# Moving a kernel's stores to ScalarE's DMA queue and its first small load to SP's queue

## The chip, the cores and the metric

The kernel runs on one core of one Trainium2 chip. A core has engines with an instruction stream each: TensorE (PE, not used here), VectorE (DVE in the profile), ScalarE (ACT), GpSimd (POOL) and SyncE (SP). Transfers between the chip's main memory (HBM) and the on-chip memory of 128 partitions are carried out by 16 DMA engines. An instruction stream issues a transfer and goes on; two of the streams issue transfers here, SP and ScalarE, and each has a DMA queue of its own. The metric is the time of one execution in microseconds (us) on the device.

## The reference

```python
def setup_inputs():
    batch, dim = 1024, 4096
    return {"x": np.random.randn(batch, dim).astype(np.float32), "axis": -1}

def reference(x, axis):
    mean = np.mean(x, axis=axis, keepdims=True)
    return ((x - mean) ** 2).astype(np.float32)
```

For each of 1024 rows of 4096 numbers the mean is taken, and each number becomes its squared distance from that mean. The input is 16.78 MB and so is the output.

## The kernel before, in words

The 1024 rows are cut into two tiles of 512 rows. In a tile each of the 128 partitions holds four whole rows (`Q = 4`), 16384 numbers or 64 KiB, which lie in one run in HBM as well. Both tiles have a buffer of their own, so no load waits for a store.

All loads are issued at the start (L46 to L53). Tile 0 comes in two transfers: the first 512 numbers of each partition (`HEAD`, 2 KiB) from ScalarE's queue on L51, the other 15872 from SP's queue on L52. Tile 1 comes in one transfer from SP's queue, right behind (L52 again).

Then a loop goes over the tiles. ScalarE takes the mean of row 3 (`mean_on_act`, L60: a scaled copy whose sum is accumulated). VectorE takes the means of rows 0, 1 and 2 (`mean_on_dve`: a reduction on L68 and a scaling of its 128 results on L71). ScalarE squares the rows in place, with the negated mean as a bias (`square_on_act`, L75), in the order 3, 0, 1 and then the first 9/16 of row 2; VectorE does the other 7/16 of row 2 in two instructions (L90 adds the negated mean, L91 squares). Last, one transfer stores the whole tile from SP's queue (L92).

The program's order is kept on each engine (`keep_in_program_order` for the instructions marked with it). SP's stream therefore is: rest of tile 0 in, tile 1 in, tile 0 out, tile 1 out. SP waits before each store until both compute engines are done with that tile. VectorE's first reduction of tile 0 waits for both transfers of that tile, since row 0 begins in the one and ends in the other; ScalarE's first mean needs only the larger. On tile 1 both wait for its one transfer.

## Time and profile before

| | |
|---|---|
| median of 3 runs (lowest, highest) | 83.39 us (83.36, 83.63) |
| profiled execution, its own time | 83.39 us |
| its span | 81.6 us |
| VectorE busy | 33.4 us (41%) |
| ScalarE busy | 34.7 us (43%) |
| bytes moved, mean rate over the span | 33.55 MB, 411 GB/s |
| tile 0: first VectorE instruction, store issued | 22.90 us, 39.85 us |
| tile 1: first VectorE instruction, store issued | 42.03 us, 59.0 us |

Times in the trace are counted from the start of the span. L12 stands for line 12 of the kernel. A name such as `x_tile<-in_x_dram` says what is written and what is read. An engine's name with a q (SPq, ACTq) is its instruction stream, where transfers are issued. In the list of DMA issues the last number is the median time from issue to landing, and landing is when all 16 DMA engines' completion writes for that transfer have arrived. In the table by stretches the columns after the length are the busy time of VectorE, ScalarE and GpSimd with the number of instructions, the granted TensorE clock, the mean busy share of the 16 DMA engines, and GB/s.

### The profile page before, as it was taken

To read this page: it belongs to the slowest core of one execution; us is meant where nothing else is said; L and a number is where in the kernel's file an instruction comes from. 1 tells how busy PE (TensorE), PEld (TensorE's weight loads), DVE (VectorE), ACT (ScalarE), POOL (GpSimd) and SP (SyncE) were. 2 spreads that over 40 slices of the span, in tenths; PEclk is the share of its full clock that TensorE was granted. 3 is DMA by queue.
4 is the path that set the end of the run, shared out by engine and by line. 5 is a ranking of instruction groups with operands and counts; after the bars stand their busy time and mean duration, and the time that the engine had idled before them with its cause. 6 is when DMAs were issued, how large, how long until landed. Compare 5 with 4: busy or idle time off the path is not lost.

```text
span 81.6 us, 83 instructions
## 1 busy us (share of the span) xinstructions
DVE 33.4 (41%) x16; ACT 34.7 (43%) x13; POOL 0.2 (0%) x4
## 2 busy tenths in 40 slices
DVE  0000000000079999999439999999800000000000
ACT  4100000000089999999339999999800000000000
POOL 0000000000000000000000000000000000000000
DMA  9099947999992999994899992999994799998590
GB/s 467 31 514 514 514 195 319 514 514 514 530 418 128 482 514 514 514 482 193 353 514 514 514 482 128 418 514 514 514 514 193 321 514 514 514 514 353 225 450 0
DMA packets 720, 33.55 MB, mean 411 GB/s; under 512 B 80, under 2 KB 80, under 8 KB 208
## 3 DMA queue, kind: packets, MB, share of 16 engines
q1 hardware_dynamic: 576, 33.29, 95.2%
q10 hardware_dynamic: 144, 0.26, 0.8%
HBM read 16.78 MB, written 16.78 MB: 411 GB/s over the span
## 4 chain that ended last, share of the span: by engine, by line
DMA 50%; DVE 21%; SPq 0%; issue 0%
DMA x_tile<-in_x_dram 50%; DVE neg_sum L68 16%; DVE x_tile L91 2%; DVE x_tile L90 1%; DVE neg_mean L71 1%; SPq L52 0%
## 5 line engine op out<-in xcount | busy, mean ns | idle before, releaser
L68 DVE TENSOR_REDUCE neg_sum<-x_tile 128x1 f32<-128x4096 f32 x6 | 26.5, 4412 | 25.1 <-DMA x_tile<-in_x_dram 25.1
L75 ACT ACTIVATE x_tile<-x_tile,neg_mean 128x4096 f32<-128x4096 f32 (+1 forms) x8 | 26.0, 3323 | 0.1
L60 ACT ACTIVATE copy<-x_tile 128x4096 f32<-128x4096 f32 x2 | 7.2, 3617 | 22.8 <-DMA x_tile<-in_x_dram 22.8
L91 DVE TENSOR_TENSOR x_tile<-x_tile 128x1792 f32<-128x1792 f32 x2 | 4.0, 2025 | 0.1
L90 DVE TENSOR_SCALAR x_tile<-x_tile,neg_mean 128x1792 f32<-128x1792 f32 x2 | 2.3, 1153 | 0.1
L60 ACT ACT_TABLE_LOAD x1 | 1.3, 1283 | 1.1 <-PEq L109 1.1
L71 DVE TENSOR_SCALAR neg_mean<-neg_sum 128x1 f32<-128x1 f32 x6 | 0.9, 154 | 0.2
L60 ACT ACTIVATION_READ_ACCUMULATOR copy<-x_tile 128x1 f32 x2 | 0.4, 186 | 0.0
L109 POOL MEMSET const-bfloat16-1.0<- 128x1 bf16 x1 | 0.1, 101 | 0.0
L109 POOL MEMSET const-uint8-127<- 128x1 uint8 x1 | 0.1, 101 | 0.0
L109 POOL MEMSET const-float32-0.0<- 128x1 f32 x1 | 0.1, 98 | 0.2 <-issue 0.2
L109 POOL MEMSET const-float32-1.0<- 128x1 f32 x1 | 0.1, 98 | 0.0
## 6 DMA issues: line engine op xcount, KB each, us to landing
x_tile<-in_x_dram SPq DMA_DIRECT2D x1, 7936.0 KB, 21.9
x_tile<-in_x_dram ACTq DMA_DIRECT2D x1, 256.0 KB, 22.1
out_dram<-x_tile SPq DMA_DIRECT2D x2, 21.7
x_tile<-in_x_dram SPq DMA_DIRECT2D x1, 40.8
```

Source lines behind the costliest of these rows:

```text
L60: nc.scalar.activation(out=copy, in_=row, func=ACT.Identity, scale=-inv_d, accum_out=neg_mean)
L68: inorder(nc.vector.reduce_sum(out=neg_sum, in_=row, axis=mybir.AxisListType.X, negate=True))
L71: inorder(nc.vector.tensor_scalar_mul(out=neg_mean, in0=neg_sum, scalar1=inv_d))
L75: inorder(nc.scalar.activation(out=part, in_=part, func=ACT.Square, bias=neg_mean, scale=1.0))
L90: nc.vector.tensor_scalar_add(out=back, in0=back, scalar1=m2)
L91: nc.vector.tensor_mul(out=back, in0=back, in1=back)
L109: nc = _bacc.Bacc("TRN2", target_bir_lowering=False, num_devices=1)
```

## The change

The 2 KiB head of tile 0 is no longer issued by ScalarE; SP issues it ahead of the rest of tile 0, so that SP's stream holds all three loads and nothing else. Both stores are issued by ScalarE in place of SP. In ScalarE's stream the store of tile 0 stands between its last activation of tile 0 and its first of tile 1; the store of tile 1 is its last instruction. As SP did, ScalarE waits before each store until VectorE's part of the tile is done.

```diff
     for i in range(ntiles):
         x_tile = io.tile([P, Q * D], F32)
-        lo = 0
-        if i == 0:
-            lo = HEAD
-            nc.scalar.dma_start(out=x_tile[:, :lo], in_=x_t[i][:, :lo])
-        nc.sync.dma_start(out=x_tile[:, lo:], in_=x_t[i][:, lo:])
+        cuts = [0, HEAD, Q * D] if i == 0 else [0, Q * D]
+        for lo, hi in zip(cuts, cuts[1:]):
+            nc.sync.dma_start(out=x_tile[:, lo:hi], in_=x_t[i][:, lo:hi])
         tiles.append(x_tile)
...
         nc.vector.tensor_mul(out=back, in0=back, in1=back)
-        nc.sync.dma_start(out=out_t[i], in_=tiles[i])
+        nc.scalar.dma_start(out=out_t[i], in_=tiles[i])
```

## The prediction

> **What bounds the kernel now.** I read the page's DMA parts first, since both compute engines are busy for only two fifths of the span (41% and 43%), then the DMA share by stretches, then the instructions in order of time, and last the packet records behind the DMA view (each DMA engine's packets with start, length, queue and size), which I tell in words. From the page, the packets, the queues and the issues:

> ```profile
> DMA packets 720, 33.55 MB, mean 411 GB/s; under 512 B 80, under 2 KB 80, under 8 KB 208
> q1 hardware_dynamic: 576, 33.29, 95.2%
> q10 hardware_dynamic: 144, 0.26, 0.8%
> x_tile<-in_x_dram SPq DMA_DIRECT2D x1, 7936.0 KB, 21.9
> x_tile<-in_x_dram ACTq DMA_DIRECT2D x1, 256.0 KB, 22.1
> out_dram<-x_tile SPq DMA_DIRECT2D x2, 21.7
> ```

> The DMA share (next to last column) in four stretches: load of tile 0, load of tile 1, store of tile 0, store of tile 1.

> ```profile
> 1.75:21.60 19.85, 0.00 (x0) 0.68 (x1) 0.00 (x0) 1.00 1.00 418
> 21.70:41.00 19.30, 16.71 (x8) 16.72 (x6) 0.00 (x0) 1.00 1.00 433
> 41.10:60.50 19.40, 16.71 (x8) 16.72 (x6) 0.00 (x0) 1.00 1.00 432
> 60.50:79.90 19.40, 0.00 (x0) 0.00 (x0) 0.00 (x0) 1.00 1.00 432
> ```

> The share is 1.00 in each: the DMA engines run from 1.75 us to the end without a gap, so the kernel is a DMA stream of 33.55 MB. It stays gapless for one reason, seen in the instructions in order of time (start, length):

> ```profile
> 39.85 0.35 SPq L92 DMA_DIRECT2D out_dram<-x_tile  x1
> 42.03 4.42 DVE L68 TENSOR_REDUCE neg_sum<-x_tile 128x1 f32<-128x4096 f32 x1 [2.25 <-DMA x_tile<-in_x_dram]
> ...
> 56.89 2.03 DVE L91 TENSOR_TENSOR x_tile<-x_tile 128x1792 f32<-128x1792 f32 x1
> 58.99 0.34 SPq L92 DMA_DIRECT2D out_dram<-x_tile  x1
> ```

> Store 0 is issued at 39.85, while load 1 still runs (its completion writes are at 41.00 to 41.56 on the sixteen engines, the last landing at 42.01). Tile 1's compute runs from 42.03 to 58.92, store 1 is issued at 59.0, and store 0's data end at 60.53 to 61.11. Store 1's descriptors thus wait about half a microsecond for the engines: that is all the slack there is. Whatever delays tile 1's landing by more than that opens a gap in the stream.

> **The change part by part.** *Head on SP's queue.* ScalarE loses a 0.39 us issue at 0.73; it then waits for data until 22.70, so this is worth nothing. SP issues the head at 0.73, the big part at about 1.11, tile 1 at about 1.5 (issues take 0.38 to 0.43). An SP issue at 0.73 had its first packet at 1.75, a lag of 1.02, so the big part could start at 2.13; the head's eight packets per engine (8 x 0.084 = 0.67) fill that time, and on one queue load 1 followed load 0 without a gap. The head's 0.67 us is paid as before, only first instead of in between. I take 0. Bounds: -0.29, if the head is wholly inside the wait (0.38 - 0.67); +0.74, if the big part pays the queue's cold start again (first 62 KB packet 3.08 against 2.34). VectorE, which waited for the head's own completion (landing 22.87, q1's 22.67), starts tile 0 0.20 earlier, at 22.70 as ScalarE does; its last instruction then ends at 39.58 instead of 39.78.

> *Store 0 on ScalarE's queue.* ScalarE's last activation of tile 0 ends at 39.45 (37.25 + 2.20). It now waits 0.13 for VectorE's 39.58, and issues the store at 39.65 (0.07 after VectorE, as SP did). Queued behind it on ScalarE is only tile 1's mean, which cannot start before 42.0; the 0.39 us issue is hidden there with 2 us to spare. SP's queue is moved past nothing: it has only loads left. What does move is the store's packets, from behind load 1 in q1 to q10, beside it. They reach the engines at 39.65 + 1.02 = 40.67 (lag of the load) or 39.65 + 1.27 = 40.92 (upper bound from the store: issued at 39.85, first packet 41.12). Load 1's last data packets end at 41.00 to 41.56, after both. So when such a packet ends it is q10's turn: a 64 KB store packet (2.46 us, first of its kind) goes ahead of load 1's 4-byte completion write, as the head's 2 KB packet did at tile 0. The first store packets ended at up to 44.16 in this trace; completion then, plus 0.45 to landing (41.56 to 42.01), is 44.61; without the 0.12 switch gap seen there it is 44.47. Tile 1 lands at about 44.54, 2.53 late. The data are there in time; only the message is late.

> *Store 1.* Tile 1's work keeps its 16.97 us from landing to issue, so the store is issued at 59.0 + 2.53 = 61.53. First packets at +1.02 on the first engine, +1.21 on fifteen and +1.44 on the last (first packets of load 0: 1.75 to 1.94, and 2.17): 62.55 to 62.97. But the engines have been empty since 60.5 to 61.1, a new gap of almost 2 us. Eight packets, 2.46 + 7 x 2.42 = 19.40, end at 82.37 on the last engine, against 80.46 now: +1.91. An idle queue's first store packet is not in the trace. Bounds: nothing more, or the load's largest cold start (3.44 - 2.34 = 1.10). I take the 0.12 of the store's own first packet, nearest in kind. The stagger's low end (no late sixteenth engine) makes the sum 1.7, the upper lag and cold start 1.91 + 0.25 + 1.06 = 3.2. The tail after the last landing (80.81 to 81.6) stays.

> *Sum*: 0 + 1.91 + 0.12 = +2.0. Span 81.6 + 2.0 = 83.6; the profiled execution is 83.39 with 1.79 around its span, equal to the median of the three runs (83.39), so 85.4 us.

> [...]

> **The rivals.** *The completion is not overtaken* (83.4, no change). For it: at tile 0 both queues had been filled long before, while here the store arrives only 0.1 to 0.9 us before load 1's data end, and an engine may have picked its next item by then. Against it: one overtaken engine of sixteen is enough, since the waiter needs all, and the latest ends (41.56) leave 0.6 us and more. Then nothing else in the stream changes.

> *The head on SP's queue starts the stream sooner, and nothing is overtaken* (83.39 - 0.29 = 83.1, faster). It decides only if small packets begin before the big transfer could, and the completion keeps its place. Against it: the first packet waited 1.02 us whatever came after.

> *ScalarE's queue starts a transfer more slowly than SP's.* The trace bounds its lag only by 1.02 and 3.93 (head issued at 0.73, its first packet at 4.66, held up by turns). From 1.91 on (41.56 - 39.65) the store comes too late to overtake, but starts late itself: nothing at that point, +2.5 at 3.93, say 84.6.

> *Two store packets go ahead of the completion*: another 2.42, 87.8. Against it: the turns at tile 0 were one for one throughout.

> **How the numbers follow.** Overtaken as described 0.74; not overtaken 0.14; sooner start 0.05; slow queue 0.04; two packets 0.03. A measurement of this kernel tells about 0.3% (0.25 us) from no change. Faster 0.05; same 0.14; slower 0.74 + 0.04 + 0.03 = 0.81. The likeliest case's own range is 83.39 + 1.7 - 0.3 = 84.8 to 83.39 + 3.2 = 86.6. That holds about 0.67 of the chance; to leave out no more than 0.2, the range goes down to 83.3 and takes in the unchanged case.

> **What would show it.** Right: the store's issue on ScalarE at about 39.65; tile 1's first VectorE and ScalarE instructions at about 44.5 instead of 42.03, waiting for the load; load 1's issue to landing at some 43 us instead of 40.8, with its bytes moved by 41.6; ScalarE's store issue at 61.5; a dip in the DMA strip near 61 to 62.5; q10 carrying 16.78 MB. Wrong: tile 1 starting at 42.0 with a gapless stream (not overtaken); tile 0 landing before 22.3 (a sooner start); a gap at 41 to 43 (slow queue); tile 1 starting near 47 (two packets).

## The result and the profile after

The changed kernel takes 83.88 us (median of 6 runs, 83.82 to 83.98), the kernel before 83.55 (6 runs, 83.36 to 83.66): a ratio of 1.0043, 95% interval 1.0027 to 1.0059. It is slower, as forecast, but by 0.4% and not by the 2.4% of the forecast 85.4 us. The likeliest case did not happen, so the direction came true by another cause than the forecast's. The profiled execution took 83.98 us with a span of 82.2.

From the page of the changed kernel, queues and DMA issues:

```profile
q10 hardware_dynamic: 288, 16.78, 48.1%
q1 hardware_dynamic: 432, 16.78, 48.0%
...
x_tile<-in_x_dram SPq DMA_DIRECT2D x1, 7936.0 KB, 21.4
x_tile<-in_x_dram SPq DMA_DIRECT2D x1, 256.0 KB, 2.8
out_dram<-x_tile ACTq DMA_DIRECT2D x2, 22.5
x_tile<-in_x_dram SPq DMA_DIRECT2D x1, 40.3
```

q10 carries the stores, so the change does what it says, and the head lands after 2.8 us in place of 22.1. Tile 1's load took 40.3 us to land. The forecast needed 43. The line that moved the wrong way is the third: a store takes 22.5 us from issue to landing where it took 21.7.

The instructions in order of time, around tile 1 of the changed kernel:

```profile
39.61 0.38 ACTq L90 DMA_DIRECT2D out_dram<-x_tile  x1
41.91 4.42 DVE L66 TENSOR_REDUCE neg_sum<-x_tile 128x1 f32<-128x4096 f32 x1 [2.38 <-DMA x_tile<-in_x_dram]
...
56.77 2.03 DVE L89 TENSOR_TENSOR x_tile<-x_tile 128x1792 f32<-128x1792 f32 x1
58.88 0.34 ACTq L90 DMA_DIRECT2D out_dram<-x_tile  x1
```

Store 0 is issued at 39.61 (forecast 39.65), tile 1 starts at 41.91 (forecast 44.5; before 42.03), store 1 is issued at 58.88. Nothing is late, and yet the span of the profiled execution is 0.6 us longer (82.2 against 81.6; the medians of the runs are 0.33 us apart). The packet records show where:

```
first store packet, 16 engines     starts          length, lowest/median/highest   ends
before                             41.12..41.69    2.451/2.459/2.466               43.58..44.16
changed kernel                     41.05..41.54    3.088/3.237/3.466               44.32..44.77
```

Load 1's data end at 41.54 in place of 41.56 on the last engine. The store's first packet then takes 3.24 us instead of 2.46, and all fifteen after it 2.418 (2.42 before). The last store data end at 80.99 against 80.46. The 0.5 us more is what is left of this longer packet after a vanished gap of 0.12 us ahead of it and some thousandths in each later packet.

So there are two questions: why was the completion write not overtaken, and what is the long first packet?

### The profile page after: what moved, and what is told of

It reads as the page before. It is cut to its first block, busy times and chain, and to the rows that moved or that the text cites. A ratio compares the mean times of both kernels' runs of the same rounds, so it can differ in the third digit from the quotient of the medians.

```text
span 82.2 us, 82 instructions
## 1 busy us (share of the span) xinstructions
DVE 33.4 (41%) x16; ACT 34.7 (42%) x13; POOL 0.2 (0%) x4
## 2 busy tenths in 40 slices
DMA packets 720, 33.55 MB, mean 408 GB/s; under 512 B 80, under 2 KB 80, under 8 KB 208
## 3 DMA queue, kind: packets, MB, share of 16 engines
q10 hardware_dynamic: 288, 16.78, 48.1%
q1 hardware_dynamic: 432, 16.78, 48.0%
HBM read 16.78 MB, written 16.78 MB: 408 GB/s over the span
## 4 chain that ended last, share of the span: by engine, by line
DMA 49%; DVE 20%; SPq 1%; issue 0%
DMA x_tile<-in_x_dram 49%; DVE neg_sum L66 16%; DVE x_tile L89 2%; DVE x_tile L88 1%; SPq L50 1%; DVE neg_mean L69 1%
## 6 DMA issues: line engine op xcount, KB each, us to landing
x_tile<-in_x_dram SPq DMA_DIRECT2D x1, 7936.0 KB, 21.4
x_tile<-in_x_dram SPq DMA_DIRECT2D x1, 256.0 KB, 2.8
out_dram<-x_tile ACTq DMA_DIRECT2D x2, 22.5
x_tile<-in_x_dram SPq DMA_DIRECT2D x1, 40.3
```

## Experiments

### The two parts, each alone

The edit of e1_stores_only, against the changed kernel, brings the head back to ScalarE's queue:

```diff
-        cuts = [0, HEAD, Q * D] if i == 0 else [0, Q * D]
-        for lo, hi in zip(cuts, cuts[1:]):
-            nc.sync.dma_start(out=x_tile[:, lo:hi], in_=x_t[i][:, lo:hi])
+        lo = 0
+        if i == 0:
+            lo = HEAD
+            nc.scalar.dma_start(out=x_tile[:, :lo], in_=x_t[i][:, :lo])
+        nc.sync.dma_start(out=x_tile[:, lo:], in_=x_t[i][:, lo:])
```

> One part alone: the stores go from ScalarE's queue, the head of tile 0 stays on ScalarE's queue as before. In the changed kernel the first store packet on each DMA engine took 3.09 to 3.47 us in place of 2.46 us, and q10 had carried nothing until then. Theory A (a queue's first use is dear): here q10 has carried the head 18 us earlier, the first store packet takes 2.42 to 2.47 us and the time is that of before, 83.4 to 83.6. Theory B (a queue that starts from empty is dear, or ScalarE's store reaches the engines late): the first store packet again takes 3.1 to 3.5 us, and the time is the changed kernel's, 83.8 to 84.0. Under both, tile 1 lands near 41.9 as in the changed kernel.

The edit of e2_head_only brings the stores back to SP's queue:

```diff
-        nc.scalar.dma_start(out=out_t[i], in_=tiles[i])
+        nc.sync.dma_start(out=out_t[i], in_=tiles[i])
```

> The other part alone: the head goes from SP's queue first, the stores stay on SP's queue. The data of load 1 ended at 41.54 on the last engine in the changed kernel and at 41.56 before, so both theories expect the time of before within 0.1 us (83.4 to 83.6); a first store packet of 2.4 to 2.5 us, behind the 0.12 us switch gap. If the head's move is itself what costs, it comes out at 83.8 to 84.0.

The stores alone: 83.54 us, ratio 1.0023 (1.0004 to 1.0043), a median between two groups: seven of twelve executions lay at 83.33 to 83.56 and five at 83.85 to 84.08. The profiled one was of the first group, and its first store packet took 2.47 us behind a gap of 0.11.

The head alone: 83.11 us, ratio 0.9951 (0.9939 to 0.9964). Neither theory had that; both said no change. Store 0 follows load 1 on q1 without the gap of before (0.12 us), and its packets take 2.418 us from the first on. The DMA issues of e2_head_only and of e1_stores_only:

```profile
x_tile<-in_x_dram SPq DMA_DIRECT2D x1, 7936.0 KB, 21.6
x_tile<-in_x_dram SPq DMA_DIRECT2D x1, 256.0 KB, 2.6
out_dram<-x_tile SPq DMA_DIRECT2D x2, 21.7
x_tile<-in_x_dram SPq DMA_DIRECT2D x1, 40.4
```

```profile
out_dram<-x_tile ACTq DMA_DIRECT2D x2, 21.8
```

A store needs 21.7 or 21.8 in both. The 22.5 exists only with both parts together, or in part of the executions. Beside the head's gain of 0.35 us (83.11 against 83.46), moving the stores as well costs 83.88 - 83.11 = 0.77 us, the size of the longer packet (3.24 - 2.42 = 0.82).

To see the second group of e1_stores_only, it was profiled twice more.

> The kernel with the stores alone moved, looked at again: of its twelve times seven lay at 83.33 to 83.56 and five at 83.85 to 84.08, and the profile was one of the first kind, with a first store packet of 2.47 us. If the first store packet's cost comes and goes from one execution to the next, this one shows either 2.47 us with a time below 83.6, or 3.1 to 3.5 us with a time above 83.8. A time above 83.8 with a short first packet would mean that the five came from something else.

> The same kernel once more, for the same question: a first store packet of 2.47 us goes with a time below 83.6, one of 3.1 to 3.5 us with a time above 83.8.

The one took 83.37 us with first store packets of 2.45 to 2.47, the other 84.14 us with a median of 3.22 (long on 14 engines of 16). In the same kernel the long packet thus came with the longer time, in three profiled executions, two short and one long. Not all of the 0.77 us between the last two is the packet's: load 1's data already ended 0.32 us later (41.80 against 41.48).

### When is a completion overtaken?

e3_early_store and e4_half_early issue store 0 earlier, by leaving out work (one execution each). The edits against the changed kernel, of e3 first:

```diff
-        square_on_act(row[2][:, :H], m2)
-        back = row[2][:, H:]
-        nc.vector.tensor_scalar_add(out=back, in0=back, scalar1=m2)
-        nc.vector.tensor_mul(out=back, in0=back, in1=back)
+        if i > 0:
+            square_on_act(row[2][:, :H], m2)
+            back = row[2][:, H:]
+            nc.vector.tensor_scalar_add(out=back, in0=back, scalar1=m2)
+            nc.vector.tensor_mul(out=back, in0=back, in1=back)
```

```diff
-        square_on_act(row[2][:, :H], m2)
-        back = row[2][:, H:]
+        cut = H // 2 if i == 0 else H
+        square_on_act(row[2][:, :cut], m2)
+        back = row[2][:, (D + H) // 2 if i == 0 else H:]
```

> The changed kernel without the squares of tile 0's row 2, so that its first store is issued near 37.2 in place of 39.61. The row is stored as it was loaded; less work is done. Load 1's last packet begins at 38.63 to 39.11 on the engines. If the store reaches the engines 1.0 to 1.3 us after its issue (38.2 to 38.5) and queues take turns, one store packet goes ahead of that last packet: tile 1 lands near 44.3, or near 46.7 if its completion write is overtaken as well. If it reaches them 2.3 to 2.7 us after (39.5 to 39.9), which is theory B's late arrival: tile 1 lands at 41.9 (completion not overtaken) or 44.3 (overtaken), and the first store packet takes 2.42 to 2.47 us. If starting from empty costs 0.7 to 1.0 us by itself, the first store packet takes 3.1 us or more here too.

> The changed kernel with half of the squares of tile 0's row 2 left out, so that its first store is issued near 38.3, 1.3 us earlier, in the middle of load 1's last packets (38.63 to 41.54). Half of that row is stored as it was loaded. Late arrival (effective 2.3 to 2.7 us after the issue): the store is there at 40.6 to 41.0, its first packet takes 2.42 to 2.5 us, and with turns per packet the completion write is overtaken, tile 1 landing near 44.3. A fixed cost of starting from empty: first packet again 3.1 to 3.5 us, whatever happens to the completion. Completion never overtaken: tile 1 lands at 41.9.

The instructions of e3_early_store in order of time, then those of e4_half_early:

```profile
37.32 0.38 ACTq L91 DMA_DIRECT2D out_dram<-x_tile  x1
45.38 3.62 ACT L58 ACTIVATE copy<-x_tile 128x4096 f32<-128x4096 f32 x1 [8.09 <-DMA x_tile<-in_x_dram]
45.38 4.42 DVE L66 TENSOR_REDUCE neg_sum<-x_tile 128x1 f32<-128x4096 f32 x1 [9.03 <-DMA x_tile<-in_x_dram]
```

```profile
38.21 0.38 ACTq L91 DMA_DIRECT2D out_dram<-x_tile  x1
42.83 4.42 DVE L66 TENSOR_REDUCE neg_sum<-x_tile 128x1 f32<-128x4096 f32 x1 [4.88 <-DMA x_tile<-in_x_dram]
```

With the earlier issue tile 1 starts at 45.38, with the later at 42.83. The records agree: in e3 load 1's data ended at 41.87 to 42.58, but 14 of the 16 completion writes came at 44.53 to 44.99, behind a whole store packet; in e4 data and completions both ended at 41.84 to 42.52. So the forecast's mechanism exists: an overtaken completion comes one store packet (2.42 us) late. e3 does less work and takes 85.67 us, and between 61.90 and 63.19 its DMA engines stand empty. What was wrong is *when* it happens: e4's store was issued 3.6 to 4.3 us before load 1's data ended, and overtook nowhere.

In e3 and e4 an extra 0.7 to 1.3 us sits in load 1's last packet (3.13 to 3.68 us instead of 2.42), and the first store packet has none of it in e3 and up to 0.47 in e4. In these two runs the cost thus followed the arrival of the second queue's packets, and was for the most part not in the store's own. None of the expectations had this, so tile 1 started at none of their times (41.9, 44.3 or 46.7 for e3, 41.9 or 44.3 for e4).

e8_between puts the issue between those two, to see at what moment an engine settles what follows a packet. Against the changed kernel:

```diff
-        square_on_act(row[2][:, :H], m2)
-        back = row[2][:, H:]
-        nc.vector.tensor_scalar_add(out=back, in0=back, scalar1=m2)
-        nc.vector.tensor_mul(out=back, in0=back, in1=back)
+        square_on_act(row[2][:, :H if i > 0 else 256], m2)
+        if i > 0:
+            back = row[2][:, H:]
+            nc.vector.tensor_scalar_add(out=back, in0=back, scalar1=m2)
+            nc.vector.tensor_mul(out=back, in0=back, in1=back)
```

> The changed kernel with only 256 of the 4096 numbers of tile 0's row 2 squared, so that its first store is issued near 37.7 (the rest of that row is stored as it was loaded). With an issue at 37.32 the completion write was overtaken on 14 of 16 engines, with one at 38.21 on none, although the store was there before the last packets ended in both. If an engine chooses what follows a packet when that packet starts, the store, which reaches the engines 1.0 to 1.36 us after its issue (38.7 to 39.1), overtakes only on the engines whose last packet starts after that (starts spread over 38.65 to 39.15): on 1 to 12 of 16, and tile 1 lands near 45.2 since one engine is enough. If the choice falls earlier, it overtakes on none and tile 1 lands at 42.4 to 42.8, held up only by q10's first use.

The instructions of e8_between in order of time:

```profile
37.76 0.38 ACTq L91 DMA_DIRECT2D out_dram<-x_tile  x1
...
45.38 4.42 DVE L66 TENSOR_REDUCE neg_sum<-x_tile 128x1 f32<-128x4096 f32 x1 [8.98 <-DMA x_tile<-in_x_dram]
```

Fourteen completion writes came at 41.96 to 42.42, two at 44.87 and 45.00, and those two hold tile 1 back as much as the fourteen of e3 did. The four issues stand in one row:

```
                 store 0    last load packets   completions   tile 1
                 issued     start               overtaken     starts
e3_early_store   37.32      38.68..39.17        14 of 16      45.38
e8_between       37.76      38.61..39.21         2 of 16      45.38
e4_half_early    38.21      38.65..38.94         0 of 16      42.83
changed kernel   39.61      38.63..39.11         0 of 16      41.91
```

This is the picture of a choice for the next item that is made about when a packet *starts*, and not when it ends. How long a store needs to reach the engines is shown by store 1 of e3, which found them empty:

```profile
62.35 0.34 ACTq L91 DMA_DIRECT2D out_dram<-x_tile  x1
```

Its first packets began at 63.19 to 63.34, 0.84 to 0.99 us after the issue. The border isn't sharp: e8's last load packets began 0.85 to 1.45 us after the issue of store 0, and two completions were overtaken; e3's began 1.35 to 1.85 us after it, and all but two were. In e8 nine of those packets began 1.1 us or more after the issue, yet only two completions were overtaken. So the choice fell some tenths of a us before the packet started (an estimate from these times), or the store needed longer to reach a busy engine; no run tells these two apart.

### What is the long first packet?

Two runs use q10 on a small scale at the start. e5_warm_all, against the changed kernel (e6_warm_half has `warm[:8]` and `x_t[0][:8, :16]`):

```diff
+    warm = ctx.enter_context(tc.tile_pool(name="warm", bufs=1)).tile([P, 16], F32)
+    nc.scalar.dma_start(out=warm[:128], in_=x_t[0][:128, :16])
+
     tiles = []
```

> The changed kernel with one small transfer more at the start, from ScalarE's queue: 64 bytes of each partition into a tile that nothing reads (8 KB in all), so that q10 has been used on every DMA engine long before the first store. If the first use of a queue costs 0.7 to 0.8 us (changed kernel: first store packet 3.24 against 2.42), the first store packet here takes 2.42 to 2.5 us and the time falls from 83.9 to that of the head alone moved, 83.0 to 83.3. If q10 costs because it is a second queue, or idle, the first store packet keeps its 3.1 to 3.5 us and the time stays at 83.8 to 84.0.

> As the run before it, with the small transfer on 8 partitions only, so that it runs on part of the 16 DMA engines. If the first use is dear on each engine by itself, the first store packet takes 2.42 to 2.5 us on the engines that the small transfer used and 3.1 to 3.5 us on the others, and the time stays at 83.8 to 84.0 because the last engine sets it. If the cost lies in the issuing engine or in the queue as a whole, all sixteen packets are short and the time is 83.0 to 83.3.

e5 takes 83.94 us, ratio 1.0056 (1.0042 to 1.0069), and its first store packet is 3.23 us in the median, long on 15 engines of 16; e6 takes 83.94 with 3.09 to 3.48 on all. It is not the first use of a queue.

e9_swapped exchanges the two queues; e10_second_store moves only store 1 to ScalarE's queue. Both edits are against the changed kernel:

```diff
-            nc.sync.dma_start(out=x_tile[:, lo:hi], in_=x_t[i][:, lo:hi])
+            nc.scalar.dma_start(out=x_tile[:, lo:hi], in_=x_t[i][:, lo:hi])
...
-        nc.scalar.dma_start(out=out_t[i], in_=tiles[i])
+        nc.sync.dma_start(out=out_t[i], in_=tiles[i])
```

```diff
-        nc.scalar.dma_start(out=out_t[i], in_=tiles[i])
+        (nc.sync if i == 0 else nc.scalar).dma_start(out=out_t[i], in_=tiles[i])
```

> The changed kernel with the two queues exchanged: all three loads from ScalarE's queue, both stores from SP's. If the 0.7 to 0.8 us of the first store packet belong to a store that comes on another queue than the load running before it, they are here too: first store packet 3.1 to 3.5 us, time 83.8 to 84.0. If they belong to ScalarE's queue or to ScalarE as the issuer of a store, the first store packet takes 2.42 to 2.5 us and the time is 83.0 to 83.3.

> The changed kernel with store 0 back on SP's queue; only store 1 goes from ScalarE's queue, so that the change of queue falls between two stores, at 60.4 to 61.0, with no load anywhere. If what costs is the beginning of a queue that was not in use, the first packet of store 1 takes 3.1 to 3.5 us and the time is 83.8 to 84.0. If it is the meeting of a load on one queue with a store on the other, it takes 2.42 to 2.5 us and the time is 83.0 to 83.3. In both, tile 1 lands near 41.9 and store 0 begins without a gap.

The DMA issues of e9_swapped, then of e10_second_store:

```profile
out_dram<-x_tile SPq DMA_DIRECT2D x2, 22.5
```

```profile
out_dram<-x_tile SPq DMA_DIRECT2D x1, 21.6
out_dram<-x_tile ACTq DMA_DIRECT2D x1, 22.5
```

e9 takes 83.93 us, ratio 1.0056 (1.0041 to 1.0071), and e10 83.99, 1.0063 (1.0046 to 1.0080). SP's queue pays as ScalarE's did (3.24 us in the median), and in e10 store 1 pays behind store 0 (3.24 us) with no load in sight. So in these runs it is neither ScalarE nor a load beside a store, but large packets on one queue following large packets on the other. Nor is it a queue that starts anew: store 1 of e3 and e8, on engines that stood empty, had first packets of 2.45 to 2.46 us.

e7_no_head is e2_head_only with `cuts = [0, Q * D]`, that is, without a head:

> Everything on SP's queue and no separate head: tile 0 in one transfer, tile 1 in one, two stores. Moving only the head to SP gave 83.11 against 83.46. If that gain comes from q10 no longer being used (no switch gap of 0.12 us before the store, store packets of 2.418 instead of 2.422), it is here too: 83.0 to 83.3. If it comes from the small packets going first, it is gone: 83.4 to 83.6.

83.25 us beside 83.50 for the kernel before, ratio 0.9976 (0.9964 to 0.9988), with gapless store packets of 2.418 us: a gain of a single queue is there without the head. Whether the head first adds to it is left open, the two having been measured beside different runs of before.

Two last runs tried what might make the change of queue cheap. e11_warm_beside is e5_warm_all without the head (`cuts = [0, Q * D]`). e12_warm_late, against the changed kernel, makes the `warm` tile as e5 does and fills it during load 1:

```diff
         square_on_act(row[3], m3)
+        if i == 0:
+            inorder(nc.scalar.dma_start(out=warm, in_=x_t[0][:, :16]))
```

> Stores from ScalarE's queue; tile 0 loaded in one transfer from SP's queue; a transfer of 64 bytes per partition from ScalarE's queue at the start into a tile that nothing reads. Its packets should go turn by turn with load 0's, to 22 us, as the head did in the kernel before, only smaller. If the alternation through load 0 is what makes the first store packet short, it is 2.42 to 2.5 us in the profile or in part of the executions, which then lie at 83.2 to 83.5; if the alternation is not it, it is 3.1 to 3.5 us in all and the time is 83.8 to 84.0.

> The changed kernel with the same tiny transfer issued from ScalarE's queue during load 1, after the first squaring (26 to 30 us). If recent use of the queue keeps the first packet short, the store's first packet takes 2.42 to 2.5 us. The tiny transfer's own first packet then takes the 0.8 us, or lengthens the load's packet beside it, so that tile 1 lands near 42.7 and the time stays near 83.9: what is moved is only the place of the cost. If a queue that changes over pays each time, the store's first packet takes 3.1 to 3.5 us as well, and the time is 84.4 to 84.8. If a tiny packet brings no cost and the store none either, the time is 83.1 to 83.4.

e11 takes 84.02 us, ratio 1.0065 (1.0051 to 1.0079). Its tiny packets went turn by turn with load 0's (they landed after 22.1 us), and the engines divided within one execution: on ten the first store packet took 2.44 to 2.47 us, on six 3.08 to 3.46, and the time was that of the long ones. That fits neither expectation: with the alternation ten engines of sixteen were short, in the changed kernel none, so it went with short packets engine by engine, and not reliably.

e12 takes 83.91 us, ratio 1.0055 (1.0040 to 1.0070), with a first store packet of 3.07 to 3.46 although q10 had been served up to that moment (the tiny transfer, issued at 26.32, landed after 15.8 us). Its tiny packets lengthened nothing (tile 1 starts at 41.98 us, in the changed kernel at 41.91), so this change of queue did not cost by itself either. None of the three expectations fits: the first store packet is that of the second, the time that of the first. Its DMA issues and instructions:

```profile
warm<-in_x_dram ACTq DMA_DIRECT2D x1, 8.0 KB, 15.8
```

```profile
26.32 0.38 ACTq L84 DMA_DIRECT2D warm<-in_x_dram  x1
39.62 0.34 ACTq L93 DMA_DIRECT2D out_dram<-x_tile  x1
```

It also answers the other question a second time. Issued at 26.32, its first packets ran at 31.36 to 31.90: they let pass not only the load packet under way (26.54 to 28.95 on the first engine) but also the next (28.95 to 31.37).

## Why the prediction was right or wrong

*What bounds the kernel*: right. The end moved only where the DMA stream did (last store data 80.99 against 80.46 us, span 82.2 against 81.6).

*The head on SP's queue*: its term of 0 is right for load 0, whose last data end at 22.21 against 22.24, and VectorE's earlier start came (22.64 against 22.90). Moved alone it gained 0.35 us, for the most part by a term that the sum did not have: with nothing on q10 the 0.12 us gap ahead of store 0 and the slightly longer store packets (2.422 us against 2.418) are gone. From the end of load 1's data to that of the last store's took 38.64 us (41.70 to 80.34) in place of 38.90 (41.56 to 80.46), which is 0.26 of the 0.35; where the rest lies is not shown. The rival "a sooner start" named a gain of 0.29, but for another reason.

*ScalarE's waiting and issuing*: right, 39.61 against 39.65, hidden before 41.91.

*"So when such a packet ends it is q10's turn"*: this is the step that failed, and the forecast's whole +2.0 us hung on it. Turns per packet are there in the runs, and so are an overtaken completion and its price (e3, e8: tile 1 at 45.38 and 85.67 us). But the store had to be there by about the time at which load 1's last packets *began*, 38.63 to 39.11; issued at 39.61 it could not. It was there before they ended, as the forecast had it: with the 0.99 us of e3's store 1, by 40.60 (an estimate), and the data ended at 41.05 to 41.54. So the rival of a slow ScalarE queue isn't the reason. At tile 0 both queues had been full since the start (both transfers issued at 0.73 us), so that trace couldn't tell a choice at the end of a packet from one at its start. The rival "not overtaken" gave just this reason and got 0.14. That the turns go by single packets held in other runs as well: in e3 and e8 overtaken completions come 2.42 us after their data, and in e12 the tiny packets run one at a time, from 31.36, 33.79 and 36.21 us, with one load packet between two of them.

*Store 1's gap*: did not arise, since tile 1 was not late.

*An idle queue's first packet*: the sum took 0.12 from the store's own first packet and named the load's cold start (up to 1.10) as the upper bound. For the case that it meant, a store that begins on empty engines, the 0.12 was not needed: store 1 of e3 and e8 had first packets of 2.45 to 2.46 us, which the sum already had. What it put at nothing is the change of queue without a gap, and store 0, not store 1, paid for that: its first packet took 0.82 us longer than those after it (3.24 against 2.42). In the rival "not overtaken", "nothing else in the stream changes" was wrong by this term, which is the measured loss. That the kernel came out slower, as forecast, is therefore luck.

What stays open is why the engines' first packet behind the other queue is 2.46 us in some executions (with the head on ScalarE's queue mostly, in e11 on ten engines) and 3.1 to 3.5 in the others. First use (e5, e6), the issuing engine (e9), the direction of the transfer (e10) and recent use (e12) were tried, and the first packet stayed long: medians of 3.23 us in e5 (short on one engine) and of 3.24 in e9 and e10, 3.09 to 3.48 in e6, 3.07 to 3.46 in e12. One thing went with it on every engine, in the kernel before, the changed kernel, e1 with its two repeats, e5, e6, e9, e11 and e12: where store 0's first packet was short (61 engines, 2.44 to 2.47 us), its next six took 2.422 to 2.427 us in the mean; where it was long (99 engines, 3.06 us and more), each of them took 2.418. The length of the first packet thus went with that of the next six; what puts an engine into the one or the other group is not shown.

## What to carry to other kernels

Two queues shared the DMA engines packet by packet here (in e12 one load packet of 2.42 us between two tiny ones), but an engine had settled its next item about a packet ahead (an estimate from the four issue times). A store on the second queue overtook the first queue's completion on no engine where it was issued 0.44 to 0.73 us before the last packets began (e4), on 2 of 16 at 0.85 to 1.45 us (e8) and on 14 at 1.35 to 1.85 us (e3); so the earlier issue made the kernel slower (85.67 against 83.88 us, with less work done). For this kernel, one gapless stream of large transfers in a fixed order, one queue was best: the head moved to SP's queue with the stores left there, 83.11 us, ratio 0.9951, beats both kernels.

## What was not expected of the hardware

- The first 64 KB packet of a queue that took over from another was 3.1 to 3.5 us long instead of 2.42 in most traces, between a load and a store and between two stores, on either queue; when the second queue's store was issued 1.4 to 2.3 us earlier, the extra sat mostly in the first queue's last packet (3.13 to 3.68 us in e3 and e4).
- Within one execution (e11) sixteen DMA engines divided into ten short and six long.
- A 64-byte packet issued on a second queue waited 5.0 us (26.32 to 31.36) behind 64 KB packets, two of them.
